# Decoder trunk on one core: sums as columns, each tile evicted at its own last product, the last three groups tile by tile, and the last 1/rms by root, reciprocal and one Newton step

## The chip, the cores and the metric

The kernel runs on one core of a Trainium2 chip. Its engines, as the profile names them, are TensorE (PE, with PEld for its weight loads), VectorE (DVE), ScalarE (ACT), GpSimd (POOL) and SyncE (SP), whose queue issues nearly all DMAs. The metric is the device time of one execution in microseconds (us), as a median of several runs.

## What is computed

Two layers of a decoder trunk over 1024 rows of width 1024, in float32. Each layer has a mixing sub-layer and a SwiGLU sub-layer of width 2816, both between two RMS norms and modulated by a vector c:

```python
c_act = jax.nn.silu(c)
for l in range(DEPTH):
    mod = c_act @ ada_w[l] + ada_b[l]
    shift_m, scale_m, gate_m, shift_f, scale_f, gate_f = [
        m[:, None, :] for m in jnp.split(mod, N_MOD, axis=-1)]

    h = rms_norm(x, g_pre_mix[l]) * (1.0 + scale_m) + shift_m
    proj = h @ w_in[l] + b_in[l]
    q, k, v, u = jnp.split(
        proj, [ATTN_WIDTH, ATTN_WIDTH + KV_WIDTH, ATTN_WIDTH + 2 * KV_WIDTH], axis=-1)
    ...
    mix = jnp.concatenate([attn_out, pool_out], axis=-1) @ w_out[l]
    x = x + gate_m * rms_norm(mix, g_post_mix[l])

    h = rms_norm(x, g_pre_ffn[l]) * (1.0 + scale_f) + shift_f
    f = (jax.nn.silu(h @ w_gate[l]) * (h @ w_up[l])) @ w_down[l]
    x = x + gate_f * rms_norm(f, g_post_ffn[l])
```

q and k are rotated in the first 16 of each head's 64 columns; attention is a sliding window of 128 with a sink per head; u goes through trailing means of 2, 4, 8 and 16 rows.

## The kernel before

**Products.** A float32 product is made of three matmuls of rounded parts: `split` (L220 on ScalarE, L221 on VectorE) makes a high part `hi` and a rest `lo`, and `mm3` multiplies hi by hi (L263), hi by lo (L266) and lo by hi (L267). A full matmul has 512 columns. The rows are worked in two halves of 512, each of four tiles of 128.

**Stages.** Mixing of a layer is u, q and kv products, rotation, attention and pooling, then `natural_proj` for w_out, which for each half of the columns (nh = 0, 1) collects four tiles in four PSUM banks over all k and evicts them at the end (L680: times G, the gate row; and a sum of squares on ScalarE, L501). In the profiled execution it lies at about 30 to 300 us for layer 0 and 985 to 1243 for layer 1. The up products (300 to 700, 1340 to 1600) and the down products (700 to 970, 1600 to 1903) use seven products `p1` to `p7` on combined blocks instead of eight. In the last layer the last down product, `p4`, goes in pairs of tiles, (0, 1) and then (2, 3); each pair runs through six groups of k, and within the last group tile by tile. `ended` is called at each tile's end and, in the last layer, calls `finish`.

**The ada stream.** The modulation `c_act @ ada_w` is spread beside these stages in steps of a few operations: `ada_sum` loads two blocks of ada_w in SP's queue and adds them, times c_act, into a tile `ada` of [128 x 512] on VectorE (L298); what is left is a sum over the 128 partitions. Before the change `ada_gate` (the gate rows: two halves for each sub-layer) and `ada_pair` (shift and scale of the second sub-layer: four parts) split the tile and multiply it by `picks`, a column of ones between zeros, so that the sum comes out as a row. The gate's row gets its bias and norm weight (two rows loaded by DMA; L471, L472) and goes to DRAM, from where `load_gate` spreads it over the partitions as `G`. The pair's rows are copied to SBUF and turned to columns by transposes. `ada_columns`, used for the first sub-layer, makes columns directly: four matmuls of 128 x 128 parts of `ada` by one column of ones (L441).

**Order.** The program is written as generators, which `run` interleaves: at each step of the main stream, so many steps of the others. From that order a scheduler builds each engine's own queue, which that engine then works in order. A DMA is issued when SP's queue gets to it.

**Norms.** `inv_rms` (L274, L275, L279 to L281) makes 1/rms on VectorE from an integer first guess and three Newton steps of three small operations each; L509 adds the two halves' sums of squares before it. `finish` (L648 in the last half) then multiplies the tile by 1/rms, adds the residual and stores it.

Of the kernel before, what the change touches and what calls it, by code (L numbers as in the profile page):

```python
# [11 lines left out]
F32 = mybir.dt.float32  # L12
# [54 lines left out]
def hybrid_decoder_kernel(  # L67
# [33 lines left out]
    SMALL = dict(junk=1, st=12, rs=8, ss=4, halo=8, rows=1, cols=2, colp=4, sk=2)  # L101
    SHARED = dict(hT=8, fn=4, raw=2, hi=3, lo=3, sa=2, sb=2, ar=2, ada=1, ph=3, G=1)
    REGIONS = dict(
        mix=dict(cfa=2, cfb=2, qkv=5, bqkv=1, uT=4, pt=2, vz=5, rt=1, qT=1, pth=2, pwh=1, pwl=1),
# [43 lines left out]
    picks = const.tile([P, 7], F32R, name="picks")  # L148
# [9 lines left out]
    pick_row = t_("rt", [P, 7])  # L158
    nc.vector.memset(pick_row, 0.0)
    nc.vector.memset(pick_row[:, 3:4], 1.0)  # L160
    nc.vector.tensor_copy(picks, pick_row)
# [26 lines left out]
    cos_t = const.tile([P, NB, RH], F32, name="cos_t")  # L188
    sin_t = const.tile([P, NB, RH], F32, name="sin_t")
# [5 lines left out]
    def rotary_angles():  # L195
# [8 lines left out]
        nc.vector.tensor_scalar(sin_t, ang, math.pi, -math.pi, op0=ALU.min, op1=ALU.max)  # L204
        nc.vector.scalar_tensor_tensor(cos_t, sin_t, -1.0, sin_t, op0=ALU.mult, op1=ALU.max)
        nc.vector.tensor_scalar(cos_t, cos_t, -1.0, math.pi / 2.0, op0=ALU.mult, op1=ALU.add)
# [78 lines left out]
    def ada_sum(l, n0, got, whole=False):  # L285
# [23 lines left out]
        if whole:  # L309
            got.append(acc)  # L310
        else:
            got += [t_("ph", [P, 512], F32R), t_("ph", [P, 512], F32R)]
            split(*got, acc)
# [3 lines left out]
    NROW = 6 * KD + 2 * KD + 4 + 4  # L317

    def load_col_rows(l):
        rows = t_("rows", [P, P])[:NROW]  # L320
        r = 0
        for src, n in (
            (ada_b[l], 6 * KD), (g_pre_mix[l], KD), (g_pre_ffn[l], KD),
            (pool_scale[l], 4), (b_in[l, QKV:INW], 4),
        ):
            nc.sync.dma_start(rows[r : r + n, :], src.rearrange("(r p) -> r p", p=P))
            r += n
        return rows

    def cols_of(rows):  # L330
        bank = msc_bank()
        nc.tensor.transpose(bank[:, :NROW], rows, ident[:NROW, :NROW])
        cols = t_("cols", [P, NROW])
        nc.vector.tensor_copy(cols, bank[:, :NROW])
        return cols
# [68 lines left out]
    def ada_pair(l, sub, cols, ab):  # L404

        held = {}

        def close(r, hi, lo):
            if r == 0:
                held["bank"] = msc_bank()  # L410
            dst, pick = held["bank"][0:4, :], picks[:, 3 - r : 7 - r]
            nc.tensor.matmul(dst, pick, hi, start=r == 0, stop=False)
            nc.tensor.matmul(dst, pick, lo, start=False, stop=r == 3)
            if r < 3:
                return
            rows = t_("ar", [P, 512])[0:4]
            nc.scalar.activation(rows, dst, AF.Copy)
            bank = msc_bank()
            for i in range(4):
                nc.tensor.transpose(bank[:, 4 * i : 4 * i + 4], rows[:, i * P : (i + 1) * P], ident[0:4, 0:4])  # L420
            tv = bank[:, 0:16].rearrange("p (i m o) -> p m o i", i=4, m=2)
            for m in range(2):
                k0 = (3 * sub + 1 - m) * KD
                nc.vector.tensor_add(
                    ab[:, m, :].rearrange("p (o i) -> p o i", o=2), tv[:, m],
                    cols[:, k0 : k0 + KD].rearrange("p (o i) -> p o i", o=2),
                )
            ada_scale(ab, sub, slice(0, KD), cols)

        return [  # L430
            (l, (3 * sub + 1 - r // 2) * D + r % 2 * 512, lambda hi, lo, r=r: close(r, hi, lo))
            for r in range(4)
        ]

    def ada_columns(l, sub, cols, ab):


        def close(r, acc):
            bank = msc_bank()
            for i in range(4):  # L440
                nc.tensor.matmul(  # L441
                    bank[:, i : i + 1], acc[:, i * P : (i + 1) * P], ones[:, 0:1], start=True, stop=True
                )
# [7 lines left out]
            (l, (3 * sub + 1 - r // 2) * D + r % 2 * 512, lambda acc, r=r: close(r, acc), True)  # L451
# [5 lines left out]
    def ada_gate(l, sub):  # L457
# [3 lines left out]
        def close(half, hi, lo):  # L461
            n0 = (3 * sub + 2) * D + half * 512
            o = slice(half * 512, half * 512 + 512)
            gb = t_("ar", [P, 512])[0:1]
            gg = t_("ar", [P, 512])[0:1]
            nc.sync.dma_start(gb, ada_b[l : l + 1, n0 : n0 + 512])
            nc.sync.dma_start(gg, (g_post_ffn if sub else g_post_mix)[l : l + 1, o])
            bank = msc_bank()
            nc.tensor.matmul(bank[0:1, :], picks[:, 3:4], hi, start=True, stop=False)
            nc.tensor.matmul(bank[0:1, :], picks[:, 3:4], lo, start=False, stop=True)  # L470
            nc.vector.tensor_add(gb, bank[0:1, :], gb)  # L471
            nc.vector.tensor_mul(gb, gb, gg)  # L472
            nc.sync.dma_start(row[:, o], gb)

        return [
            (l, (3 * sub + 2) * D + half * 512, lambda hi, lo, half=half: close(half, hi, lo))
# [157 lines left out]
    def finish(h, t, fn, ss, G, xt=None):  # L634
# [4 lines left out]
        rstd = inv_rms(ss[:, 2 * t : 2 * t + 2])  # L639
# [13 lines left out]
    def natural_proj(fn, left, wsrc, ss, G):  # L653
# [7 lines left out]
        for nh in range(2):  # L661
            cs = slice(nh * 512, (nh + 1) * 512)
            banks = [acc_bank() for _ in range(NT)]
            for k in range(K):
# [10 lines left out]
                for t in range(NT):  # L675
                    mm3(banks[t], lh[:, tiles[t]], ll[:, tiles[t]], wh, wl, k == 0, k == K - 1)
                yield
            for t in range(NT):
                square_sum(ss, t, nh, banks[t])
                nc.vector.tensor_mul(fn[t][:, cs], banks[t], G[:, cs])  # L680
# [73 lines left out]
    def u_pass(l, h, hT, cols, uts, piece_read, ask):  # L754
        banks = [acc_bank() for _ in range(4)]
        for k in range(KD):
# [5 lines left out]
            yield  # L762
        for g in range(4):
# [10 lines left out]
            uts.append(ut)  # L774

    def att_rotary(blk, qkv):
        rot = qkv[:, 0:QK].rearrange("p (n d) -> p n d", d=HD)
        t1 = rot[:, :, 0:RH]
        t2 = rot[:, :, RH:ROT]
        nr = NH + NKV  # L780
        cb = cos_t[:, blk : blk + 1, :].to_broadcast([P, nr, RH])
        sbc = sin_t[:, blk : blk + 1, :].to_broadcast([P, nr, RH])
        tmp = t_("rt", [P, 4, nr, RH])
        nc.vector.tensor_mul(tmp[:, 0], t1, cb)
        nc.vector.tensor_mul(tmp[:, 1], t2, sbc)
        nc.vector.tensor_mul(tmp[:, 2], t2, cb)
        nc.vector.tensor_mul(tmp[:, 3], t1, sbc)
        nc.vector.tensor_sub(t1, tmp[:, 0], tmp[:, 1])
        nc.vector.tensor_add(t2, tmp[:, 2], tmp[:, 3])
# [444 lines left out]
    def down(l, wd, load, kept, fn, ended, last, prelude):  # L1234
# [47 lines left out]
        def products(name, g, lh, ll, rights, banks, ts, evict):  # L1282
# [3 lines left out]
            for some in [range(n)] if whole else [(i,) for i in range(n)]:  # L1286
                for t in ts:
                    sl = tiles[t - ts[0]]
# [37 lines left out]
        for ts in ((0, 1), (2, 3)) if last else (range(NT),):  # L1326
            banks = {t: acc_bank() for t in ts}
            for g, (p0, p1) in enumerate(DOWN_GROUPS):
# [308 lines left out]
```

## Time and profile before

| | us |
|---|---|
| median of 3 runs | 1912.27 (1906.89, 1912.27, 1913.08) |
| profiled execution | 1915.26 |
| its span | 1913.5 |
| granted clock of TensorE, mean | 0.993 |
| ScalarE busy | 946.4 (49%) |
| moved by DMA | 341.86 MB, mean 179 GB/s |

The span runs from the first to the last event that the profiler saw; the execution's time has a little around it. Busy time is counted by instruction. A matmul's row in the timeline has a duration of 0.39 us, but the next one starts before it ends, so the pitch between starts is what counts. In the views of waits a row names the engine, the tile and line that waited, and behind the arrow the engine, tile and line that it waited for; then the total, the number of waits and the longest. A half-clock stretch is one in which the profile shows the granted clock at 0.50.

### The profile page before, as it was taken

The numbers are of one execution on the slowest core, as the hardware profiler recorded it, in microseconds if no ns is written. First come the engines' busy times: TensorE is split into PE (matmuls) and PEld (weight loads), VectorE is DVE, ScalarE is ACT, GpSimd is POOL, SyncE is SP. The second block draws the span as 40 slices with busy tenths as digits, with TensorE's granted clock in tenths as the row PEclk, the third lists the DMA queues.
The fourth block names the chain that finished last, engine by engine and source line by source line (L and its number), as shares of the span: only waits on it lengthen the run. The fifth ranks groups of instructions, "written<-read, shape, count | busy, mean of one in ns | idle before, by whom it ended". The sixth has DMA issues, their size and how long they took to land.

```text
span 1913.5 us, 26037 instructions
## 1 busy us (share of the span) xinstructions
PE 1866.0 (98%) x8954; PEld 1541.1 (81%) x8954; DVE 1541.9 (81%) x2913; ACT 946.4 (49%) x1786; POOL 20.4 (1%) x67
## 2 busy tenths in 40 slices
PE   7999999999999999999999989999999999999997
PEld 5887788888878788888888868888887887888886
DVE  7899886678788888788878988846888888877687
ACT  4875795553222223445548667845622222244452
POOL 0000000000000000000000000000000000000000
PEclk9999999999999999999999989999999999999999
DMA  9345563555555655944554464536754566574342
GB/s 343 108 144 161 160 220 127 187 182 192 183 180 187 206 206 172 320 144 149 175 175 138 125 179 165 177 110 211 218 181 149 197 211 201 198 251 150 114 152 102
DMA packets 229540, 341.86 MB, mean 179 GB/s; under 512 B 17016, under 2 KB 126472, under 8 KB 229408
## 3 DMA queue, kind: packets, MB, share of 16 engines
q1 hardware_dynamic: 228800, 338.10, 53.6%
q10 hardware_dynamic: 576, 2.10, 0.3%
q8 instruction: 70, 1.15, 0.2%
q14 instruction: 62, 0.51, 0.1%
q0 software_dynamic: 32, 0.00, 0.0%
HBM read 267.25 MB, written 72.89 MB: 178 GB/s over the span
## 4 chain that ended last, share of the span: by engine, by line
PE 77%; DVE 12%; DMA 5%; ACT 3%; issue 2%; SPq 0%; DVEq 0%; ACTq 0%; POOL 0%; POOLq 0%
PE acc L263 24%; PE acc L266 23%; PE acc L267 23%; DMA ar<-in_ada_w_dram 2%; DVE lo L221 2%; DMA raw<-in_w_up_dram 2%; DVE ada L298 1%; PE msc L893 1%; PE msc L561 1%; ACT hi L220 1%; DVE fn L1151 1%; PE pv L263 1%; PE pv L266 1%; ACT raw L554 1%; DMA ar<-x 1%
## 5 line engine op out<-in xcount | busy, mean ns | idle before, releaser
L220 ACT ACTIVATE hi<-raw 128x1024 fp32r<-128x1024 f32 (+1 forms) x388 | 331.9, 868 | 364.9 <-PE acc L266 198.8
L221 DVE TENSOR_TENSOR lo<-raw,hi 128x1024 fp32r<-128x1024 f32 (+1 forms) x388 | 379.9, 986 | 121.6 <-ACT hi L220 117.4
L263 PE MATMUL acc<-t,hi 128*128 128x512 f32 x704 | 275.1, 391 | 5.8 <-ACT hi L220 5.8
L266 PE MATMUL acc<-t,hi 128*128 128x512 f32 x704 | 274.7, 390 | 0.0
L267 PE MATMUL acc<-t,lo 128*128 128x512 f32 x704 | 272.1, 390 | 0.1
L263 PE MATMUL acc<-bh,hi 128*128 128x512 f32 x520 | 202.9, 390 | 0.0
L267 PE MATMUL acc<-bh,lo 128*128 128x512 f32 x520 | 202.4, 389 | 0.0
L263 PE MATMUL acc<-hT,hi 128*128 128x512 f32 x480 | 190.2, 396 | 0.6 <-DVE fn L680 0.6
L266 PE MATMUL acc<-hT,hi 128*128 128x512 f32 x480 | 188.4, 393 | 0.0
L267 PE MATMUL acc<-hT,lo 128*128 128x512 f32 x480 | 187.5, 391 | 0.0
L1151 DVE TENSOR_TENSOR fn<-acc,fn 128x512 f32<-128x512 f32 x220 | 150.3, 684 | 39.4 <-PE acc L267 39.1
L263 PEld LDWEIGHTS acc<-t,hi 128*128 128x128 f32 x704 | 132.4, 188 | 35.3 <-ACT hi L220 8.2
L267 PEld LDWEIGHTS acc<-t,lo 128*128 128x128 f32 x704 | 132.4, 188 | 29.3 <-DVE lo L221 1.5
L266 PEld LDWEIGHTS acc<-t,hi 128*128 128x128 f32 x704 | 132.5, 188 | 27.2
L266 PE MATMUL acc<-ph,hi 128*128 128x512 f32 x320 | 124.7, 390 | 0.0
L1087 ACT ACTIVATE fn<-fn 128x512 f32<-128x512 f32 x44 | 27.8, 633 | 185.7 <-DVE fn L1151 185.7
L298 DVE SCALAR_TENSOR_TENSOR ada<-ar,c_act,ada 128x512 f32<-128x512 f32 x140 | 104.5, 746 | 12.5 <-DMA ar<-in_ada_w_dram 11.3
L267 PEld LDWEIGHTS acc<-bh,lo 128*128 128x128 f32 x520 | 97.6, 188 | 20.4
L263 PEld LDWEIGHTS acc<-bh,hi 128*128 128x128 f32 x520 | 97.6, 188 | 20.2 <-ACT sb L1249 0.2
L263 PE MATMUL acc<-hi 128*128 128x512 f32 x256 | 103.6, 410 | 2.4 <-DVE fn L680 2.0
L263 PEld LDWEIGHTS acc<-hT,hi 128*128 128x128 f32 x480 | 90.2, 188 | 19.2 <-DVE fn L680 1.4
L267 PEld LDWEIGHTS acc<-hT,lo 128*128 128x128 f32 x480 | 90.1, 188 | 18.6 <-issue 0.2
(315 smaller groups left out, 3813.5 us busy)
## 6 DMA issues: line engine op xcount, KB each, us to landing
ar<-in_ada_w_dram SPq DMA_DIRECT2D x160, 256.0 KB
raw<-in_w_gate_dram SPq DMA_DIRECT2D x44, 512.0 KB
raw<-in_w_up_dram SPq DMA_DIRECT2D x44, 512.0 KB
raw<-in_w_in_dram SPq DMA_DIRECT2D x80, 256.0 KB
raw<-keeps SPq DMA_DIRECT2D x40, 512.0 KB
keeps<-fn SPq DMA_DIRECT2D x66, 256.0 KB
two_b<-in_w_down_dram SPq DMA_DIRECT2D x30, 512.0 KB
raw<-keepa SPq DMA_DIRECT2D x25, 512.0 KB
```

Of the source, the lines that this page charges most:

```text
L220: a = nc.scalar.activation(hi, src, AF.Copy)
L221: v = nc.vector.tensor_sub(lo, src, hi.bitcast(F32))
L263: ins = nc.tensor.matmul(dst, lh, rh, start=first, stop=False)
L266: nc.tensor.matmul(dst, lh, rl, start=False, stop=False)
L267: return nc.tensor.matmul(dst, ll, rh, start=False, stop=last)
L298: ins = nc.vector.scalar_tensor_tensor(acc, w, c_act[:, i : i + 1], acc, op0=ALU.mult, op1=ALU.add)
L554: nc.scalar.activation(hf, bank, AF.Identity, bias=shift, scale=scale)
L561: ins = nc.tensor.transpose(bank[:, t * P : (t + 1) * P], src[t], ident)
L893: nc.tensor.transpose(bank[:, i * P : (i + 1) * P], s[:, ii, ck * P : (ck + 1) * P], ident)
L1087: nc.scalar.activation(g, g, AF.Silu)
L1151: nc.vector.tensor_add(halves_of(dst)[m], bank, halves_of(src)[m])
```

## The change

1. **Sums as columns.** `ada_gate` and the second sub-layer's parts now use `column_sums` (the four one-column matmuls). The gate's bias and norm weight come as columns out of `cols`, which grows by 16 rows; the product is a [128 x 4] tile `gc`, written to the DRAM row by a DMA whose elements are of 4 bytes. `picks`, `ada_pair`, its transposes and the gate's two row loads go. `ada_stream` calls a part's closing one step later than before.
2. **Evictions.** `natural_proj` evicts each tile right behind its own last product; `u_pass` evicts ahead of its last step's end.
3. **Rotation.** Two products of [128 x 10 x 16] and two sums instead of four products of [128 x 10 x 8] and two sums; the tables of sine and cosine hold each value twice. `vz` has four buffers instead of five.
4. **The last product.** In the last layer the last three groups of each pair of tiles run tile by tile.
5. **The last 1/rms.** In the last half the first column half's share, with epsilon, is prepared ahead (`ahead`); `inv_rms_ahead` takes a root on ScalarE, a reciprocal and one Newton step on VectorE.

```diff
+    def column_sums(acc):
+        bank = msc_bank()
+        for i in range(4):
+            nc.tensor.matmul(
+                bank[:, i : i + 1], acc[:, i * P : (i + 1) * P], ones[:, 0:1], start=True, stop=True
+            )
+        return bank[:, 0:4]
...
-        def close(half, hi, lo):
-            n0 = (3 * sub + 2) * D + half * 512
-            o = slice(half * 512, half * 512 + 512)
-            gb = t_("ar", [P, 512])[0:1]
-            gg = t_("ar", [P, 512])[0:1]
-            nc.sync.dma_start(gb, ada_b[l : l + 1, n0 : n0 + 512])
-            nc.sync.dma_start(gg, (g_post_ffn if sub else g_post_mix)[l : l + 1, o])
-            bank = msc_bank()
-            nc.tensor.matmul(bank[0:1, :], picks[:, 3:4], hi, start=True, stop=False)
-            nc.tensor.matmul(bank[0:1, :], picks[:, 3:4], lo, start=False, stop=True)
-            nc.vector.tensor_add(gb, bank[0:1, :], gb)
-            nc.vector.tensor_mul(gb, gb, gg)
-            nc.sync.dma_start(row[:, o], gb)
+        def close(half, acc):
+            bank = column_sums(acc)
+            k0 = (3 * sub + 2) * KD + 4 * half
+            g0 = 8 * KD + 8 + sub * KD + 4 * half
+            gc = t_("gc", [P, 8])[:, 0:4]
+            nc.vector.tensor_add(gc, bank, cols[:, k0 : k0 + 4])
+            nc.vector.tensor_mul(gc, gc, cols[:, g0 : g0 + 4])
+            nc.sync.dma_start(row[0, half * 512 : half * 512 + 512].rearrange("(i p) -> p i", p=P), gc)
...
     def ada_stream(jobs):
-        for l, n0, close, *whole in jobs:
+        ending = None
+        for l, n0, close in jobs:
             got = []
-            yield from ada_sum(l, n0, got, *whole)
-            close(*got)
+            for i, _ in enumerate(ada_sum(l, n0, got)):
+                yield
+                if ending and i == 0:
+                    ending()
+            ending = lambda close=close, got=got: close(*got)
+        yield
+        if ending:
+            ending()
...
                 for t in range(NT):
                     mm3(banks[t], lh[:, tiles[t]], ll[:, tiles[t]], wh, wl, k == 0, k == K - 1)
+                    if k == K - 1:
+                        square_sum(ss, t, nh, banks[t])
+                        nc.vector.tensor_mul(fn[t][:, cs], banks[t], G[:, cs])
                 yield
-            for t in range(NT):
-                square_sum(ss, t, nh, banks[t])
-                nc.vector.tensor_mul(fn[t][:, cs], banks[t], G[:, cs])
...
+        rot = qkv[:, 0:QK].rearrange("p (n d) -> p n d", d=HD)[:, :, 0:ROT]
...
+        tmp = t_("rt", [P, 2, nr, ROT])
+        nc.vector.tensor_mul(tmp[:, 0], rot, cb)
+        nc.vector.tensor_mul(tmp[:, 1], rot, sbc)
...
-                products(name, g, lh, ll, kept4[g], banks, ts, evict)
+                if last and g >= len(DOWN_GROUPS) - 3:
+                    final.append((g, lh, ll))
+                else:
+                    products(name, g, lh, ll, kept4[g], banks, ts, evict)
                 for _ in range(n):
                     yield
+
+            for t in ts:
+                for g, lh, ll in final:
+                    products(name, g, lh, ll, kept4[g], banks, (t,), evict, ts[0])
...
+    def inv_rms_ahead(s0, ahead):
+        a, r, y, z = (t_("rs", [P, 8])[:, :1] for _ in range(4))
+        nc.vector.scalar_tensor_tensor(a, s0, 1.0 / D, ahead, op0=ALU.mult, op1=ALU.add)
+        nc.scalar.activation(r, a, AF.Sqrt)
+        nc.vector.reciprocal(y, r)
+        nc.vector.scalar_tensor_tensor(z, y, -0.5, a, op0=ALU.mult, op1=ALU.mult)
+        nc.vector.tensor_mul(z, z, y)
+        nc.vector.scalar_tensor_tensor(y, z, 1.5, y, op0=ALU.add, op1=ALU.mult)
+        return y
```

Three places in VectorE's queue, in the kernel's line numbers before and after. Removed lines shift the numbers: L298 becomes L296, L680 becomes L661, L221 becomes L219, L1151, L1172 and L1196 become L1136, L1157 and L1181, L1571 becomes L1569, and L648 becomes L630.

The first is the end of the program, from the eviction of the last pair of tiles on (`sb` is the tile, `ss` the sums of squares, `rs` the small tiles of 1/rms). Before:

```order
L1246 TENSOR_TENSOR sb<-acc,sb 128x512 x2
L1571 TENSOR_TENSOR sb<-sb,G 128x512
L509 TENSOR_REDUCE rs<-ss 128x1
L274 TENSOR_SCALAR rs<-rs 128x1
L1571 TENSOR_TENSOR sb<-sb,G 128x512
L275 TENSOR_SCALAR rs<-rs 128x1
L279 SCALAR_TENSOR_TENSOR rs<-rs 128x1
L509 TENSOR_REDUCE rs<-ss 128x1
L280 TENSOR_TENSOR rs<-rs 128x1
L274 TENSOR_SCALAR rs<-rs 128x1
L281 SCALAR_TENSOR_TENSOR rs<-rs 128x1
```

After, the last tile, behind the last operation of the tile ahead of it:

```order
L630 SCALAR_TENSOR_TENSOR sb<-sb,rs,hT 128x512 x2
L1231 TENSOR_TENSOR sb<-acc,sb 128x512
L1569 TENSOR_TENSOR sb<-sb,G 128x512
L608 SCALAR_TENSOR_TENSOR rs<-ss,st 128x1
L610 RECIPROCAL rs<-rs 128x1
L611 SCALAR_TENSOR_TENSOR rs<-rs 128x1
L612 TENSOR_TENSOR rs<-rs 128x1
L613 SCALAR_TENSOR_TENSOR rs<-rs 128x1
L630 SCALAR_TENSOR_TENSOR sb<-sb,rs,hT 128x512 x2
```

The two tiles' small operations stood in turns; now one tile is complete before the other's eviction, and five small operations stand between eviction and last product.

The second is the change from nh = 0 to nh = 1 in layer 1's `natural_proj` (`fn` is the evicted tile, `acc` the PSUM bank, L298 a step of the ada stream, L843 and L219 parts of attention). Before:

```order
L221 TENSOR_TENSOR ph<-msc,pth 128x512
L298 SCALAR_TENSOR_TENSOR ada<-ar,c_act,ada 128x512
L832 TENSOR_TENSOR hi<-qkv,hi 128x4x64
L680 TENSOR_TENSOR fn<-acc,G 128x512 x2
L298 SCALAR_TENSOR_TENSOR ada<-ar,c_act,ada 128x512
L680 TENSOR_TENSOR fn<-acc,G 128x512
L298 SCALAR_TENSOR_TENSOR ada<-ar,c_act,ada 128x512
L680 TENSOR_TENSOR fn<-acc,G 128x512
L221 TENSOR_TENSOR lo<-raw,hi 128x512
```

After (L415 adds the bias to four columns that the ones make):

```order
L296 SCALAR_TENSOR_TENSOR ada<-ar,c_act,ada 128x512
L661 TENSOR_TENSOR fn<-acc,G 128x512
L415 TENSOR_TENSOR colp<-msc,cols 128x4
L661 TENSOR_TENSOR fn<-acc,G 128x512
L294 TENSOR_SCALAR ada<-ar,c_act 128x512
L843 ISA sb,st<-msc,mask 128x256
L843 ISA st 128x1
L843 ISA sb,st<-msc,mask 128x256
L843 ISA st 128x1
L219 TENSOR_TENSOR ph<-msc,pth 128x512
L296 SCALAR_TENSOR_TENSOR ada<-ar,c_act,ada 128x512
L661 TENSOR_TENSOR fn<-acc,G 128x512 x2
```

The first two evictions now stand ahead of an ada step and of a block of attention, and the last two behind it.

The third is the second half of the gate in layer 0's up stage (L1151 adds a product's bank to a tile, L1172 combines a block of weights in `raw`). Before:

```order
L298 SCALAR_TENSOR_TENSOR ada<-ar,c_act,ada 128x512
L1088 TENSOR_TENSOR fn<-fn 128x512
L1172 TENSOR_TENSOR raw<-raw 128x8x128
L1196 TENSOR_TENSOR fn<-fn 128x512
L1151 TENSOR_TENSOR fn<-acc,fn 128x512
L221 TENSOR_TENSOR ph<-ada,ph 128x512
```

After:

```order
L296 SCALAR_TENSOR_TENSOR ada<-ar,c_act,ada 128x512
L1073 TENSOR_TENSOR fn<-fn 128x512
L1136 TENSOR_TENSOR fn<-acc,fn 128x512
L1181 TENSOR_TENSOR fn<-fn 128x512
L1157 TENSOR_TENSOR raw<-raw 128x8x128
L1136 TENSOR_TENSOR fn<-acc,fn 128x512
L435 TENSOR_TENSOR gc<-msc,cols 128x4
L436 TENSOR_TENSOR gc<-gc,cols 128x4
```

L1181 and one L1136 have moved ahead of L1157, and the split of the sum (L221) is gone; the two small operations of the gate stand a place later.

More of the change, by code (lines that the diff above doesn't have):

```diff
@@ L185, in hybrid_decoder_kernel @@
     nc.scalar.activation(c_act, c_raw, AF.Silu)
-    cos_t = const.tile([P, NB, RH], F32, name="cos_t")
-    sin_t = const.tile([P, NB, RH], F32, name="sin_t")
+    cos_t = const.tile([P, NB, 2, RH], F32, name="cos_t")
+    sin_t = const.tile([P, NB, 2, RH], F32, name="sin_t")
     ang = t_("pt", [P, NB, RH])
@@ L308, in ada_sum @@
                 yield
[L309 to L313, printed above, removed]
+        got.append(acc)
         yield
-    NROW = 6 * KD + 2 * KD + 4 + 4
+    NROW = 6 * KD + 2 * KD + 4 + 4 + 2 * KD
     def load_col_rows(l):
@@ L1556, in hybrid_decoder_kernel @@
         ss = [t_("ss", [P, 8]) for _ in range(NHALF)]
-        tail = []
+        tail, aheads = [], []
         def ended(name, t):
```

106 lines of the change are left out of this document (39 added, 67 removed).

## The prediction

> **What bounds the kernel now.** I read the page's busy shares first.
>
> ```profile
> PE 1866.0 (98%) x8954; PEld 1541.1 (81%) x8954; DVE 1541.9 (81%) x2913; ACT 946.4 (49%) x1786; POOL 20.4 (1%) x67
> ```
>
> TensorE is busy for 98% of the span, so work taken off another engine pays only where TensorE stands still or runs slower. Next come the view of TensorE's waits (total, times, longest) and the windows of the two mixing stages in which the ada stream runs (us, PE, PEld, DVE, ACT, POOL busy, granted clock, DMA).
>
> ```profile
> PE msc L332 <- DVE ident L152: 11.1, 1, 11.1
> PE acc L263 <- ACT hi L220: 6.1, 5, 2.1
> PE msc L893 <- DVE sb L883: 3.8, 7, 0.9
> PE acc L263 <- DVE fn L680: 2.6, 5, 0.8
> PE msc L412 <- ACT ph L220: 1.9, 2, 1.8
> PE msc L814 <- DVE rt L787: 1.7, 1, 1.7
> PE msc L835 <- DVE fn L680: 1.4, 1, 1.4
> ```
>
> ```profile
> 157.00:200.00 43.00, 38.45 (x187) 29.83 (x186) 39.41 (x101) 26.25 (x61) 0.79 (x2) 0.92 0.59 172
> 1098.00:1142.00 44.00, 39.17 (x184) 30.34 (x184) 40.56 (x104) 27.80 (x69) 1.35 (x2) 0.91 0.59 173
> ```
>
> The waits are short and spread. In the two windows VectorE is busier than TensorE, 39.41 and 40.56 us, and the clock falls to 0.92 and 0.91. The same windows cut small, of TensorE alone, show why:
>
> ```profile
> 164.76:168.17 3.41, 3.31 (x13) 0.50 0.49 141
> 195.48:198.89 3.41, 2.94 (x10) 0.50 0.45 111
> 536.81:540.22 3.41, 3.41 (x9) 0.50 0.03 4
> 1106.84:1110.25 3.41, 3.41 (x10) 0.50 0.55 159
> 1137.56:1144.38 6.82, 6.01 (x15) 0.50 0.64 174
> 646.00:650.00 4.00, 2.86 (x13) 1.00 0.57 197
> ```
>
> Stretches of 3.41 us run at half clock, one after each of the longest waits (L412, L680, a first gate's L220, L814, L835), the one at 1137.56 twice as long. Each 3.41 us costs 1.7. At 646, where TensorE stood still for 1.14 of 4 us, the clock stayed 1.00: a stall of about 1.4 is near the point from which half clock follows.
>
> **The change part by part.** The sum is against the profiled execution, 1915.26 us (span 1913.5), 3.0 above the median 1912.27; the difference is then carried to the median.
>
> *The tail.* The timeline after the last matmuls (start, duration):
>
> ```profile
> 1902.24 0.39 PE L266 MATMUL acc<-two_b,hi 128*128 128x512 f32 x1
> 1902.47 0.39 PE L267 MATMUL acc<-two_b,lo 128*128 128x512 f32 x1
> 1902.90 0.69 DVE L1246 TENSOR_TENSOR sb<-acc,sb 128x512 f32<-128x512 f32 x1 [0.67 <-PE acc L267]
> 1903.68 0.63 ACT L501 ACTIVATE junk<-sb 128x512 bf16<-128x512 f32 x1 [0.64 <-DVE sb L1246]
> 1904.22 0.19 ACT L501 ACTIVATION_READ_ACCUMULATOR junk<-sb 128x1 f32 x1
> ...
> 1908.31 0.15 DVE L279 SCALAR_TENSOR_TENSOR rs<-rs 128x1 f32<-128x1 f32 x1
> 1908.50 0.16 DVE L280 TENSOR_TENSOR rs<-rs 128x1 f32<-128x1 f32 x1
> 1908.89 1.42 DVE L648 SCALAR_TENSOR_TENSOR sb<-sb,rs,hT 128x512 f32<-128x512 f32 x2
> ```
>
> ```profile
> L874 ACT ACTIVATE st<-st 128x4 f32<-128x4 f32 x32 | 6.5, 203 | 2.2 <-DVE st L873 1.9
> ```
>
> Matmuls follow each other at 0.23. The sum of squares is read out at 1904.41, the last product ends at 1910.31, and between them lie the small operations of two tiles, 0.19 apart. After: three hand-offs between engines of 0.09 (add's end 1903.59 to square 1903.68), five small DVE operations at 0.19, a root at 0.20 (the 128x4 ACT row), then 1.42: 1904.41 + 0.27 + 0.95 + 0.20 + 1.42 = 1907.25, 3.1 earlier. The other tile's last product ends 18 matmuls (six products of three), 4.1 us, ahead instead of six, 1.4, so its own chain of about 4.4 ends some 0.3 after the last matmul and can delay the last add; I take **−2.7** (bounds −3.1, and 0 if the two chains still meet). The root needs a table load, which has one row here:
>
> ```profile
> L185 ACT ACT_TABLE_LOAD x1 | 1.3, 1283 | 7.3 <-DMA rows<-in_g_pre_ffn_dram 7.3
> ```
>
> It falls at the first root, two tiles earlier, hidden by TensorE's matmuls; uncovered it costs 1.3.
>
> *TensorE's work.* The picks go: 32 matmuls of 512 columns at 0.23 are 7.3 us. 64 one-column matmuls come, priced by the like ones of the first modulation, a row of the chain:
>
> ```profile
> 790.86 0.79 PE msc L441 x8
> ```
>
> 0.099 each, 6.3 in all: **−1.0**, with the small transposes that go too.
>
> *The mixing stages.* VectorE and ScalarE lose the split of each ada sum and the two row operations of each gate:
>
> ```profile
> L221 DVE TENSOR_TENSOR ph<-ada,ph 128x512 fp32r<-128x512 f32 x16 | 11.0, 685 | 0.9 <-ACT ph L220 0.7
> L471 DVE TENSOR_TENSOR ar<-msc,ar 1x512 f32<-1x512 f32 x8 | 5.4, 674 | 0.8 <-PE msc L470 0.8
> ```
>
> A gate half on VectorE was 0.69 + 2 × 0.67 (L472 is as large as L471) = 2.03 and becomes two small operations, 0.38: 1.65 less. What reaches the end is the waits. L412's longest is 1.8; its sums now need no cast, but the new matmuls stand directly behind the same products, so part of the hand-off stays: **−1.5** (0 to −1.9). The evictions of mix_out at 1134:
>
> ```profile
> 1134.52 1.28 DVE L680 TENSOR_TENSOR fn<-acc,G 128x512 f32<-128x512 f32 x2
> 1135.72 0.74 DVE L298 SCALAR_TENSOR_TENSOR ada<-ar,c_act,ada 128x512 f32<-128x512 f32 x1
> ```
>
> Two such ada steps, 0.7 each, stand between the four evictions (the order shows the second, behind the third eviction), for which TensorE waits 2.6 + 1.4 (L263 and L835 on L680). After, each tile is evicted as soon as its own last product is done, while the next tile's three matmuls (0.69) run; in layer 1 attention work still stands between. I take half, **−2.0** (0 to −4.0). If the stalls fall below about 1.4, the half-clock stretches behind them go: of five in mixing (the double one counted as two) I take two, **−3.4** (0 to −8.5). The rotation's four products before L814's wait are these:
>
> ```profile
> 1101.83 0.24 DVE L784 TENSOR_TENSOR rt<-qkv,cos_t 128x80 f32<-128x80 f32 x1
> 1101.98 0.23 DVE L785 TENSOR_TENSOR rt<-qkv,sin_t 128x80 f32<-128x80 f32 x1
> ```
>
> Four at 0.15 become two of double width, some 0.23 each by the slope to the 0.69 of 512 columns, and two sums a piece follow unchanged: **−0.4** at L814 (0 to −1.7). A loss at these places would need a new wait, and the order shows new ones only at the write and in the up stages, below. VectorE's relief of some 5 us per stage (two gate halves at 1.65 and part of four splits at 0.69) also shortens other short waits (L893's 3.8): **−0.8** (0 to −3.8). The earlier u eviction hides in L263's wait and the vz buffer less beside TensorE's work; both nothing.
>
> The Trainium skill, "TensorE: Matmul & The Clock Gate", section "HAM oscillation — how this bites in real kernels", gives as its rule "no PE-idle gaps >~3.4µs". By it no stall here, the longest being 2.1, would cost clock, the sum would lose its −3.4 and give −4.5, 1907.8. The trace disagrees: half-clock stretches stand behind stalls of 1.4 to 2.1.
>
> *The gate write.* Four halves in mixing, whose write to DRAM was one row and becomes 512 elements of 4 bytes:
>
> ```profile
> 129.74 1.44 DMA gate<-ar
> DVE pos_f L196 <- DMA pos_i<-in_positions_dram: 5.3, 1, 5.3
> 136.00 0.75 DVE L298 SCALAR_TENSOR_TENSOR ada<-ar,c_act,ada 128x512 f32<-128x512 f32 x1 [1.10 <-DMA ar<-in_ada_w_dram]
> ```
>
> The order puts it on SP's queue ahead of the next ada load, so VectorE's wait of 1.10 grows; VectorE saves 1.65 there. I take +0.25 a half, **+1.0** (0 by the relief; 5.3, the 4-byte position load's wait, less 1.44, +3.9 a half, by the nearest small-element row). The Trainium skill, "DMA: Bandwidth & Descriptors", "Specifications", wants transfers of at least 512 B, since below that the engines do read-modify-write. It speaks against this edit; this trace has no 4-byte write.
>
> *The up stages.* At the second gate:
>
> ```profile
> 646.60 0.68 DVE L1196 TENSOR_TENSOR fn<-fn 128x512 f32<-128x512 f32 x1
> 647.21 0.68 DVE L1151 TENSOR_TENSOR fn<-acc,fn 128x512 f32<-128x512 f32 x1
> ```
>
> L1172 (now L1157), just ahead of these, prepares weights whose split TensorE waits for. L1196 and L1151, 0.61 apart, move ahead of it: 1.2 in each layer, **+2.4** (0 if the wait has slack, +5.8 if each stall also costs 1.7 of clock). The first gate's order is unchanged.
>
> *The head.* Four more small DVE operations before ident, for which TensorE waits 11.1:
>
> ```profile
> 10.78 0.22 DVE L152 CAST ident<-G 128x128 fp32r<-128x128 f32 x1
> ```
>
> Four half as wide as this row, which is 0.22, overlapping in part: I take **+0.5** (0.4, half of each, to 0.9, all of it); nothing covers them.
>
> *The sum:* +0.5 − 2.7 − 1.0 − 1.5 − 2.0 − 3.4 − 0.4 − 0.8 + 1.0 + 2.4 = −7.9: 1907.4 against the profiled execution, **1904.4** against the median.
>
> **The rivals.** *S, the waits only move:* VectorE stays near 40 of 43 us and another short wait takes each place; only tail, head and TensorE's work come in: −2.7 + 0.5 − 1.0 = −3.2, with +2.4 up to −0.8: 1911.5. *G, all of it:* the stalls of L412, L814 and L680/L835 and all five half-clock stretches go. For it: each stretch has its stall. −1.9 − 1.7 − 4.0 − 8.5, less tail and work 3.2, plus 2.4 is −16.9 to −20: about 1895. *L, slower:* the 4-byte write holds SP's queue for the time of the position load, +3.9 at two of four mixing halves, and the up stage's later weights cost clock too, +5.8, against −3.2 with no mixing gain: about +10.6, 1923. It decides from a write of 3.1 us, today's 1.44 and VectorE's relief of 1.65.
>
> **How the numbers follow.**
> The forecast has 0.50, S 0.30, G 0.10, L 0.10. S is strong because VectorE was the releaser of most waits and stays busy; G needs every hand-off to work; L needs a price that no row shows. The forecast's own range is 1898 (four windows go) to 1909 (none, and the up stage costs more). The range reaches from G's edge to S with the spread of the runs: 1894 to 1914; L is left out, and a tenth at the edges. Measurement tells 0.3%, 5.7 us, from no change: faster means below 1906.5. That is G, most of the forecast (0.39 of 0.50) and a little of S (0.03): 0.52. Same: the rest of the forecast and S, 0.38. Slower: L, 0.10.
>
> **What would show it.** Tail: last matmul to last product 4.7 us instead of 7.45, with no table load behind the last matmul. Mixing: L412's wait gone, and no row after 1.8 from the new sums; TensorE's waits on the evictions under 2; fewer stretches at 0.50 in 157–200 and 1098–1142, PEclk there above 0.92. Gate write: its landing time on the chain, and VectorE's longest wait for an ada load, 1.10 now; over 3 is L. Up: TensorE's stalls near 646 and its twin in layer 1 longer by 1.2; half clock behind them adds 1.7 each. Head: ident 0.5 later. The prediction is wrong if the half-clock stretches stay in number though the waits before them shrink, or if new ones come in the up or down stages, or if the write is over 3 us.

## The result

The changed kernel took 1940.7 us (median of 4 runs, 1939.44 to 1942.17); before, beside it, 1910.18. The ratio is 1.0161, with a 95% interval of 1.0138 to 1.0183: 30.5 us slower, where 1904.4 was forecast. Its profiled execution has a span of 1937.7 us at a mean granted clock of 0.989.

The page's busy times, and the view of TensorE's waits, of the changed kernel (line numbers are up to 38 lower than before; L261, L264, L265 are the three matmuls of a product):

```profile
PE 1878.3 (97%) x9042; PEld 1558.4 (80%) x9042; DVE 1523.6 (79%) x2848; ACT 937.1 (48%) x1773; POOL 19.4 (1%) x67
PE msc L878 <- DVE sb L868: 12.9, 7, 6.0
PE acc L261 <- ACT hi L218: 7.9, 7, 2.6
PE msc L878 <- DVE st L843: 4.2, 1, 4.2
PE msc L799 <- DVE hi L794: 2.6, 2, 1.4
```

VectorE and ScalarE have less to do, as expected, and TensorE is busy for longer, 1878 us instead of 1866. But attention's transpositions (L878), which waited 0.9 at most, now wait 6.0 and 4.2 for VectorE. VectorE in turn waits for data, and SP for the gate write (the views of VectorE's and SP's waits):

```profile
DVE ada L296 <- DMA ar<-in_ada_w_dram: 28.3, 24, 5.9
DVE raw L1151 <- DMA raw<-in_w_up_dram: 23.2, 14, 7.4
SPq L446 <- DMA gate<-gc: 24.9, 4, 7.9
```

Before, the first two were these, and SP's waits for a gate write came to 2.9 us, 0.8 at most:

```profile
DVE ada L298 <- DMA ar<-in_ada_w_dram: 11.3, 18, 1.3
DVE raw L1166 <- DMA raw<-in_w_up_dram: 11.5, 7, 2.7
```

One such place, layer 1's first gate half, in the chain (start, duration, what) and in windows (us, TensorE busy, clock, DMA share, GB/s). The gate write (L437) is issued at 1043.94, an ada load right behind it:

```profile
1042.11 0.80 PE msc L403 x8
...
1044.43 9.88 DMA ar<-in_ada_w_dram
```

```profile
1040.00:1045.00 5.00, 5.00 (x35) 1.00 0.45 141
1046.00:1054.00 8.00, 5.37 (x33) 1.00 0.57 40
```

For 8 us the core's whole traffic falls from 141 to 40 GB/s while its DMA engines are busy for more of the time (0.57 instead of 0.45). A load of 256 KB takes 9.88 us, where the median of the 160 ada loads is 3.3, and TensorE stands still for 2.63 of 8 us. It is the place where rival L has its loss; the price is the question.

### The profile page after: what moved, and what is told of

It is laid out like the page before. It is cut to its first block, busy times and chain, and to the rows that moved or that the text cites. A ratio compares the mean times of both kernels' runs of the same rounds, so it can differ in the third digit from the quotient of the medians.

```text
span 1937.7 us, 26100 instructions
## 1 busy us (share of the span) xinstructions
PE 1878.3 (97%) x9042; PEld 1558.4 (80%) x9042; DVE 1523.6 (79%) x2848; ACT 937.1 (48%) x1773; POOL 19.4 (1%) x67
## 4 chain that ended last, share of the span: by engine, by line
PE 76%; DVE 11%; DMA 7%; ACT 3%; issue 2%; SPq 1%; DVEq 0%; ACTq 0%; POOL 0%; POOLq 0%
PE acc L261 23%; PE acc L265 23%; PE acc L264 23%; DMA raw<-in_w_up_dram 3%; DMA ar<-in_ada_w_dram 2%; DVE lo L219 2%; PE msc L878 1%; ACT hi L218 1%; PE msc L532 1%; DVE ada L296 1%; DVE fn L1136 1%; DMA ar<-x 1%; PE msc L403 1%; PE pv L261 1%; PE pv L264 1%
## 5 line engine op out<-in xcount | busy, mean ns | idle before, releaser
L219 DVE TENSOR_TENSOR lo<-raw,hi 128x1024 fp32r<-128x1024 f32 (+1 forms) x388 | 380.3, 986 | 121.1 <-ACT hi L218 118.5
L261 PE MATMUL acc<-t,hi 128*128 128x512 f32 x704 | 277.0, 394 | 7.2 <-ACT hi L218 7.2
L265 PE MATMUL acc<-t,lo 128*128 128x512 f32 x704 | 274.8, 393 | 2.7 <-DVE lo L219 2.6
L264 PE MATMUL acc<-t,hi 128*128 128x512 f32 x704 | 275.8, 392 | 0.0
L261 PE MATMUL acc<-bh,hi 128*128 128x512 f32 x520 | 202.9, 390 | 0.0
L265 PE MATMUL acc<-bh,lo 128*128 128x512 f32 x520 | 202.5, 389 | 0.0
L261 PE MATMUL acc<-hT,hi 128*128 128x512 f32 x480 | 190.9, 398 | 2.5 <-ACT uT L749 2.0
L264 PE MATMUL acc<-hT,hi 128*128 128x512 f32 x480 | 188.3, 392 | 0.0
L265 PE MATMUL acc<-hT,lo 128*128 128x512 f32 x480 | 187.8, 392 | 0.0
L1136 DVE TENSOR_TENSOR fn<-acc,fn 128x512 f32<-128x512 f32 x220 | 150.2, 683 | 42.7 <-PE acc L265 42.3
L261 PEld LDWEIGHTS acc<-t,hi 128*128 128x128 f32 x704 | 133.3, 189 | 36.9 <-ACT hi L218 9.8
L265 PEld LDWEIGHTS acc<-t,lo 128*128 128x128 f32 x704 | 133.3, 189 | 32.8 <-DVE lo L219 4.9
L264 PEld LDWEIGHTS acc<-t,hi 128*128 128x128 f32 x704 | 133.3, 189 | 27.7
L296 DVE SCALAR_TENSOR_TENSOR ada<-ar,c_act,ada 128x512 f32<-128x512 f32 x140 | 104.5, 746 | 28.8 <-DMA ar<-in_ada_w_dram 28.3
L264 PE MATMUL acc<-ph,hi 128*128 128x512 f32 x320 | 124.7, 390 | 0.0
L265 PEld LDWEIGHTS acc<-bh,lo 128*128 128x128 f32 x520 | 97.7, 188 | 20.3
L261 PEld LDWEIGHTS acc<-bh,hi 128*128 128x128 f32 x520 | 97.7, 188 | 20.0
L261 PEld LDWEIGHTS acc<-hT,hi 128*128 128x128 f32 x480 | 90.4, 188 | 21.0 <-ACT uT L749 2.4
L265 PEld LDWEIGHTS acc<-hT,lo 128*128 128x128 f32 x480 | 90.1, 188 | 18.6
L264 PEld LDWEIGHTS acc<-hT,hi 128*128 128x128 f32 x480 | 90.4, 188 | 16.4
```

Of the source, the lines that this page charges most:

```text
L219: v = nc.vector.tensor_sub(lo, src, hi.bitcast(F32))
L261: ins = nc.tensor.matmul(dst, lh, rh, start=first, stop=False)
L264: nc.tensor.matmul(dst, lh, rl, start=False, stop=False)
L265: return nc.tensor.matmul(dst, ll, rh, start=False, stop=last)
L296: ins = nc.vector.scalar_tensor_tensor(acc, w, c_act[:, i : i + 1], acc, op0=ALU.mult, op1=ALU.add)
L1136: nc.vector.tensor_add(halves_of(dst)[m], bank, halves_of(src)[m])
```

## The experiments

Each run is compared with the kernel before on the same chip. The times are medians; the ratio on record can differ a little from their quotient (for e6 0.9977 against 0.9982):

| run | us | before beside it | ratio (95%) |
|---|---|---|---|
| change | 1940.7 | 1910.18 | 1.0161 (1.0138 to 1.0183) |
| e1 gate as rows | 1911.74 | 1909.07 | 1.0015 (1.0006 to 1.0025) |
| e2 write on ScalarE's queue | 1944.65 | 1909.07 | 1.0176 (1.0153 to 1.0198) |
| e3 elements of 16 B | 1913.56 | 1909.07 | 1.0025 (1.0011 to 1.0039) |
| e4 write twice | 1949.14 | 1909.07 | 1.0207 (1.0192 to 1.0222) |
| e5 all but the columns | 1907.19 | 1910.0 | 0.9981 (0.9972 to 0.9991) |
| e6 tail only | 1906.54 | 1910.0 | 0.9977 (0.9967 to 0.9986) |
| e7 columns only, gate as rows | 1913.2 | 1910.0 | 1.0015 (1.0006 to 1.0024) |
| e9 e1 and a spare write, near | 1935.1 | 1910.59 | 1.0128 (1.0110 to 1.0147) |
| e10 e1 and a spare write, far | 1911.92 | 1910.59 | 1.0014 (1.0000 to 1.0029) |
| e11 tail, late picks | 1911.68 | 1910.59 | 1.0006 (0.9996 to 1.0016) |
| e12 e5, late picks | 1912.79 | 1910.59 | 1.0017 (1.0007 to 1.0026) |
| e13 e1, closing at once | 1918.94 | 1909.4 | 1.0051 (1.0035 to 1.0066) |
| e14 tail and rotation | 1905.07 | 1909.4 | 0.9977 (0.9967 to 0.9987) |
| e15 tail and evictions | 1908.53 | 1909.4 | 0.9994 (0.9986 to 1.0003) |

### The gate write: e1 to e4

```diff
-            nc.sync.dma_start(row[...].rearrange("(i p) -> p i", p=P), gc)
+            # e1, one step of the stream later
+            nc.tensor.transpose(bank[0:4, 0:P], gc, ident)
+            nc.scalar.activation(gr, bank[0:4, 0:P], AF.Copy)
+            nc.sync.dma_start(row[...].rearrange("(i p) -> i p", p=P), gr)
+            # e2
+            nc.scalar.dma_start(row[...].rearrange("(i p) -> p i", p=P), gc)
+            # e3
+            nc.sync.dma_start(row[...].rearrange("(p i) -> p i", i=4), gc)
+            # e4
+            nc.sync.dma_start(row[...].rearrange("(i p) -> p i", p=P), gc)
+            nc.sync.dma_start(spare[...].rearrange("(i p) -> p i", p=P), gc)
```

> The changed kernel, with the gate's four columns turned back into rows (one transposition on TensorE, one copy on ScalarE, a step of the ada stream later), so that each half goes to DRAM as 4 elements of 512 B instead of 512 of 4 B. Theory W (the write of 4-byte elements holds back the core's DMAs for about 8 us, eight times): the stalls and half-clock stretches at 112, 671, 1051, 1087 and 1608 to 1634 us, some 36 us with their clock, go; 1902 to 1910 us. Theory O (the new order of VectorE's work and the later closings make the loss, the write only marks the places): within 4 us of the changed kernel, 1936 to 1942.

> The changed kernel, with the 4-byte write issued from ScalarE's queue instead of SP's. Theory W1 (the write slows all transfers of the core while it lasts): ada and weight loads are as late as before, DMA falls to some 20 GB/s for about 7 us after each write, 1933 to 1942 us. Theory W2 (only what is queued behind the write on the same queue waits for it): the mixing stalls go and only the G loads' own wait for the write in the two up stages stays, 1905 to 1920 us. Theory O: 1936 to 1942.

> The changed kernel, with the gate written as 128 elements of 16 B for each half instead of 512 of 4 B; the gate's columns then stand in another order, so the output is that of a permuted gate. Theory W, priced by the element: a write takes about 2 us of held transfers instead of 8, 1906 to 1916 us. Theory W, priced by what an element of under 512 B costs at all (a fixed latency): near the changed kernel, 1930 to 1942. Theory O: 1936 to 1942.

> The changed kernel, with each 4-byte write made a second time into a spare row of DRAM. Theory W: the slow stretch after each write grows from about 8 to about 16 us; at least as much again is lost as the writes cost now, 1965 to 1990 us. Theory O: only a little more traffic, 1938 to 1946.

e1 takes 29.0 us off (1940.7 to 1911.74; 27.9 by the ratios), 1.7 above theory W's range, and theory O falls. e2 keeps the whole loss (1944.65, 2.7 above every range it was given): another queue does not help, so it isn't what stands behind the write on SP's queue. Its traffic falls as in the change:

```profile
1040.00:1045.00 5.00, 5.00 (x35) 1.00 0.42 134
1046.00:1054.00 8.00, 6.75 (x38) 1.00 0.23 34
```

Its engines are busy for only 0.23 of the second window, so part of that fall is that less was asked for; but its ada load takes 9.18 us there, much as in the change. e3 is near e1: 128 elements of 16 B cost little. e4 misses: a second write adds 8.4 us, not 30. Its trace shows why: the two writes are issued 0.44 us apart (1050.35 and 1050.79), and the ada load behind them takes 11.13 us instead of 9.88. They overlap, and the slow stretch grows by little.

### What in the write is slow: e9 and e10

Both are e1, with a write that nothing reads:

```diff
             nc.vector.tensor_mul(gc, gc, cols[:, g0 : g0 + 4])
+            # e9
+            nc.sync.dma_start(spare[0:512].rearrange("(i p) -> p i", p=P), gc)
+            # e10
+            nc.sync.dma_start(spare.rearrange("(i p s) -> p i s", p=P, s=64)[:, :, 0], gc)
```

> The first experiment's kernel (gate as rows, 1911.7 us) with one thing added: each gate half's columns are also written as 512 elements of 4 B, side by side, into a spare row that nothing reads. Theory W1 (such a write slows all transfers of the core while it lasts): most of the loss comes back although no G load waits for it, 1925 to 1938 us. If the loss came from the G loads that waited for the write on SP's queue: 1912 to 1918.

> As the run beside it, but the 512 elements stand 256 B apart in the spare buffer. Theory L (neighbouring elements lie in the same line of memory, and partial writes to one line wait for each other): the write is harmless, 1911 to 1916 us. Theory C (each small element costs its time wherever it goes): as the run beside it, within 4 us.

e9 brings 23.4 us of the loss back (1935.1 against 1911.74; 21.6 by the ratios) though no G load waits for it. e10 moves the same 512 elements of 4 B, 256 B apart, in as many DMA packets (233845 on both pages), and its median has no cost that can be measured, though four of its ten runs took 1916 to 1922 us where e1's highest is 1914.6. Windows from some 2 us after the first write on and behind layer 1's first write, of e9 and then of e10:

```profile
109.00:117.00 8.00, 5.16 (x31) 1.00 0.61 39
1046.00:1054.00 8.00, 5.80 (x35) 1.00 0.61 45
```

```profile
106.80:114.80 8.00, 8.00 (x52) 1.00 0.75 224
1034.80:1042.80 8.00, 8.00 (x49) 1.00 0.63 182
```

The same windows behind the other writes agree: at seven of the eight e10 moves 180 to 244 GB/s, where e9 moves 38 to 63 and the change 9 to 61. At the eighth, layer 0's second half in mixing, e10 too moves only 34, with its DMA engines busy for 0.13: little is asked for there.

So 512 elements of 4 B do not by themselves hold the traffic back; they do where neighbours go to neighbouring addresses, and e3 shows that a quarter as many, four times as large, do so far less. That they meet in one line of memory and wait for each other there was argued, not shown: the runs show that the distance decides, not where the wait is, and no distance between 4 and 256 B was tried.

### The columns, and a second trace of before: e5, e7, e8

e5 has the parts 2 to 5 of the change on the kernel before (but five `vz` buffers still), e7 has part 1 with the write of e1 and the four `vz` buffers, and e8 is the kernel before.

> The kernel before with all of the change but the sums as columns: evictions, rotation, tail. Theory P (a sum as columns costs TensorE 0.8 us, since the trace shows eight records for one closing and not two closings: 16 closings are 13 us against 7.3 for the picks that go, some +6 to +8 net, and that ate what the other parts give): 1901 to 1906 us where before is about 1909. Theory N (the columns are worth as much in waits as they cost, and the other parts give nothing but the tail): 1906 to 1908.

> The kernel before with the sums as columns alone, the gate written as rows of 512 B (as in the first experiment). Theory P: TensorE's one-column matmuls add some 15 us and the picks' 7.3 go, waits fall by some 3 to 4: 1912 to 1916 us. Theory N: 1908 to 1911.

> The kernel before once more, for a second trace. If the half-clock stretches of mixing belong to fixed stalls, they stand at the same places (165, 195, 537, 1107, 1138 us); if they depend on where a stall falls against the clock's own windows, some are gone or elsewhere, the execution is nearer to 1909 than the 1915.26 that was profiled, and the sum that was made against the profiled execution counted a chance as a gain.

e7 is where theory P has it, 2.9 us slower (0.15% of 1910; one of its 12 runs took 10672.91 us, which does not move the median); e5 is where theory N has it, 3.6 us faster and no more than the tail alone (e6, below). So the columns do cost, and the other parts bring nothing beside the tail. The two do not add up: e1, which has all parts, is at 1.0015 as e7 is, so beside the columns the 3.6 us of the other parts do not show. Against e5 the columns cost 6.5 us (1.0015 less 0.9981), and why it is 2.9 in one place and 6.5 in the other was not found. The chain's row of the changed kernel above has eight matmul records for one closing of four sums, and its groups of instructions have this row:

```profile
L403 PE MATMUL msc<-ones_r,ada 128*128 128x1 f32 x160 | 19.2, 242 | 1.3 <-DVE ada L296 1.3
```

Of the 160 records 32 are layer 1's first modulation, as before; 128 are new, where 64 were forecast.

e8 shows the other error. Windows as in the prediction, of TensorE alone (e8, then before's at its first gate):

```profile
157.00:200.00 43.00, 37.77 (x185) 1.00 0.61 178
525.00:545.00 20.00, 18.65 (x82) 1.00 0.58 195
1098.00:1142.00 44.00, 38.35 (x177) 0.96 0.63 182
...
1134.56:1137.97 3.41, 3.40 (x8) 0.50 0.57 149
```

```profile
525.00:545.00 20.00, 17.88 (x72) 0.91 0.41 135
```

The same program, with nearly the same stalls in the two mixing windows (at the first gate TensorE stands still for 1.35 us instead of 2.12), has one half-clock stretch ahead of its last matmul in this trace (1134.56), where the first trace had the time of six. Its span is 1908.6 us, 4.9 less.

### The other parts alone: e6, e14, e15

```diff
# e6: only inv_rms_ahead, ahead, final and t0 of the change
# e14: e6, and the rotation's tables and operations
# e15: e6, and in natural_proj
                 for t in range(NT):
                     mm3(banks[t], lh[:, tiles[t]], ll[:, tiles[t]], wh, wl, k == 0, k == K - 1)
+                    if k == K - 1:
+                        square_sum(ss, t, nh, banks[t])
+                        nc.vector.tensor_mul(fn[t][:, cs], banks[t], G[:, cs])
```

> The kernel before with the tail alone: the last three groups tile by tile, and 1/rms by root, reciprocal and one Newton step. Both theories: from last matmul's start to the span's end 8.9 us instead of 11.0, so 2.1 us less, 1906 to 1908 us; a regrouping that cost TensorE a wait would give 1909 or more.

> The kernel before with the tail and the rotation in four operations. If the rotation gives what the prediction said (0.4 us) or nothing: 1905.5 to 1908, not to be told from the tail alone. If it gives more and the evictions take it back: 1901 to 1905.

> The kernel before with the tail and each tile of the output product evicted at its own last product. If the evictions give nothing: 1905 to 1908.5 us. If they cost what the rotation gives: 1908 to 1911. If they give the 2 us and half-clock stretches of the prediction: 1900 to 1904.

The tail gives 0.23% (2.7 to 6.3 us), the rotation nothing beside it by the ratios (its median lies between its two ranges), and the evictions take 3.2 back (0.9994 less 0.9977, of 1910; the one interval begins where the other ends, so this is just clear of the noise). The timeline of VectorE in e15 at layer 0's change from nh = 0 to nh = 1, and then in e6:

```profile
191.66 0.75 DVE L298 SCALAR_TENSOR_TENSOR ada<-ar,c_act,ada 128x512 f32<-128x512 f32 x1
192.33 0.42 DVE L820 TENSOR_TENSOR hi<-qkv,hi 128x256 fp32r<-128x256 f32 x1
192.91 0.75 DVE L298 SCALAR_TENSOR_TENSOR ada<-ar,c_act,ada 128x512 f32<-128x512 f32 x1 [0.16 <-DMA ar<-in_ada_w_dram]
193.58 2.48 DVE L690 TENSOR_TENSOR fn<-acc,G 128x512 f32<-128x512 f32 x4
...
195.97 0.74 DVE L298 SCALAR_TENSOR_TENSOR ada<-ar,c_act,ada 128x512 f32<-128x512 f32 x1
```

```profile
191.30 1.28 DVE L691 TENSOR_TENSOR fn<-acc,G 128x512 f32<-128x512 f32 x2
192.50 0.74 DVE L298 SCALAR_TENSOR_TENSOR ada<-ar,c_act,ada 128x512 f32<-128x512 f32 x1
```

In e15 ScalarE's square of the first bank starts at 191.65, so the bank is done, but VectorE comes to it at 193.58, behind two ada steps that stand ahead of it in its queue. The evictions are in one piece and no earlier. The view of TensorE's waits of e15 has them:

```profile
PE acc L263 <- DVE fn L690: 2.8, 4, 1.9
```

In e6 the like row has the same total, 2.8, over five waits of at most 0.8; here the longest is 1.9. This shows why nothing was gained; the loss itself is spread over e15's trace in pieces of 1 to 2 us, and was not traced to one wait.

### When a sum is closed: e11 to e13

```diff
# e11 (e6), e12 (e5): split one step later, picks another step later
+            for i, _ in enumerate(ada_sum(l, n0, got)):
+                yield
+                if rest:
+                    rest()
+                    rest = None
+                if ending and i == 0:
+                    rest = ending()
# e13 (e1): no delay
-                if ending and i == 0:
-                    write = ending()
+            write = close(*got)
```

> The tail alone (1906.5 us) and the closings of the ada sums spread over two later steps: the split one step later, the picks another step later, the sums still as rows. If the five stalls of 1.0 to 1.8 us at the closings (160, 643, 1470 and the like) come from work that reaches the engines' queues right behind the sum: 1900 to 1904 us. If VectorE's load sets them, they move: 1905 to 1908.

> All of the change but the columns (1907.2 us), with the same late split and picks. If evictions and rotation give something once the closings no longer stall: 1898 to 1902 us, under the run beside it. If they give nothing, as they did without it: within 2 us of the run beside it.

> The first experiment's kernel (all of the change, gate as rows, 1911.7 us) with each sum closed as soon as it is complete, as before the change, instead of one step later. If the late closing costs the columns what it cost the picks: 1905 to 1908 us. If not: 1910 to 1914.

e11 and e13 miss; e12 stays within 2 us of e11. By the ratios, closing later costs the picks 5.5 and 6.9 us (e11 against e6, 1.0006 less 0.9977; e12 against e5, 1.0017 less 0.9981), and closing at once costs the columns 6.9 (e13 against e1, 1.0051 less 1.0015). In e11 TensorE waits 2.8 us for the split of the late sums, and the two waits are up to 1.7 long:

```profile
PE msc L466 <- DVE ph L221: 2.8, 2, 1.7
```

The change's own delay was right for the columns. Why it is worth that much was not followed further.

## Why the prediction was wrong

**The gate write: +1.0 forecast, 28 to 29 measured.** The step that failed is "I take +0.25 a half". It priced the write by how long its own successor waits and set VectorE's relief against it, and its upper end was the position load, 5.3 us. e2 and e9 show that the write slows the core's transfers for about 8 us, and not just what is queued behind it. The eight halves reach TensorE at five places (112, 672, 1051, 1087 and 1634 us), where the prediction counted four halves in mixing and none in the up stages. Of the 28.1 us that the change's span is above e1's, TensorE stands still for 17.5 (59.4 against 41.9) and is busy for 10.6 more (1878.3 against 1867.7), at mean granted clocks of 0.989 and 0.995: the four longest of these stalls are each followed by a stretch at half clock, which the prediction's term for the write did not have either. The G load waits for the write at all four sub-layers, 5.1 to 7.9 us each, and in the up stages it holds the loads of w_gate and w_up, on SP's queue behind it:

```profile
649.80 0.37 SPq L437 DMA_DIRECT2D gate<-gc  x1
658.10 0.32 SPq L446 DMA_DIRECT2D G<-gate  x1
658.52 0.39 SPq L1119 DMA_DIRECT2D raw<-in_w_gate_dram  x1
```

That may be the 5.6 us that are left of the loss (29.0 less e9's 23.4; 6.3 by the ratios), which no run has by itself. Rival L had the right edit and place, and its sign came in: VectorE's longest wait for an ada load is 5.9 us, over 3. But it had only 0.10, its time was 18 too low, and its mechanism, that the write holds SP's queue, is not the one: e2 loses as much from ScalarE's queue. That "this trace has no 4-byte write" should have given the edit a wide range. The Trainium skill, "DMA: Bandwidth & Descriptors", "Specifications", has transfers under 512 B done by read-modify-write. e10 agrees only in part: 512 elements of 4 B, 256 B apart, have no cost that its median shows.

**TensorE's work: −1.0 forecast, +5.5.** The row "790.86 0.79 PE msc L441 x8" was read as two closings; it is one, with two records for each sum. 128 records at 0.10 are 12.8 us, less 7.3 for the picks: +5.5. The whole of part 1 measures +2.9 (e7) or +6.5 (e1 against e5), so whether the columns earn anything back in waits stays open.

**Waits at the closings: −1.5 forecast, and VectorE's relief, −0.8.** L412's wait of 1.9 is gone and the new matmuls wait 1.3, no row of them over 1.8, as the prediction's sign has it:

```profile
PE msc L403 <- DVE ada L296: 1.3, 2, 1.0
```

That is 0.6 less in this trace; in e1's they wait 0.4, which is 1.5 less. No run has either term by itself.

**Half-clock stretches: −3.4 forecast, nothing to earn.** The profiled execution, 1915.26, lay above all 19 runs of before in the first experiments' comparison (1905.35 to 1911.42), and five stretches in mixing were part of that. e8 has stalls at 160, 190, 1098 and 1132 us too, with one stretch, and e1 still has the time of four in mixing (at 165, at 195, twice as long, and at 1107). They were priced as if each belonged to its stall; by these two traces a stall only risks one. The Trainium skill ("TensorE: Matmul & The Clock Gate", "HAM oscillation — how this bites in real kernels") has as its rule that TensorE's gaps stay under some 3.4 us. Neither trace fits it, since e8's one stretch also stands behind stalls under 2 us (waits of 0.76 and 0.99).

**Evictions: −2.0 forecast, +3.2** (e15 against e6). The step "each tile is evicted as soon as its own last product is done" took each eviction to come as soon as the code has it; at run time VectorE's queue was behind. In the change itself TensorE's waits on the evictions are 1.3 us where they were 4.0, under 2 as the prediction's sign has it, and no time came of it.

**Rotation: −0.4 forecast, 0** by the ratios (e14 against e6), inside what can be told.

**Up stages: +2.4 forecast, about 0.** Without the write (e1) the stall at 645 is there, 1.7 us instead of 1.1 before, but the one at 1586, 1.3 before, is gone. In the change it is there, at 1608, just ahead of the last write.

**Tail: −2.7 forecast; the mechanism right, 2.05 in the trace.** Before, last matmul's start to last product's end is 1910.31 − 1902.47 = 7.84. After, it is 1934.53 − 1928.74 = 5.79 (from that matmul's end 5.40, where the prediction has 4.7):

```profile
1928.44 1.41 DVE L630 SCALAR_TENSOR_TENSOR sb<-sb,rs,hT 128x512 f32<-128x512 f32 x2
1928.74 0.39 PE L265 MATMUL acc<-two_b,lo 128*128 128x512 f32 x1
1929.77 0.68 DVE L1231 TENSOR_TENSOR sb<-acc,sb 128x512 f32<-128x512 f32 x1
...
1931.30 0.69 DVE L1569 TENSOR_TENSOR sb<-sb,G 128x512 f32<-128x512 f32 x1 [0.85 <-ACT junk L472]
1931.91 0.15 DVE L608 SCALAR_TENSOR_TENSOR rs<-ss,st 128x1 f32<-128x1 f32 x1
1932.33 0.16 DVE L610 RECIPROCAL rs<-rs 128x1 f32<-128x1 f32 x1 [0.27 <-ACT rs L609]
...
1933.11 1.42 DVE L630 SCALAR_TENSOR_TENSOR sb<-sb,rs,hT 128x512 f32<-128x512 f32 x2
```

Two things are later than the sum has them. The last add (L1231) starts 1.03 behind the last matmul's start instead of 0.43, behind the other tile's last product (L630), a delay that the prediction named and took too small. And the working left out that L1569 overwrites the tile that the square reads, so it waits for the square, and stands ahead of L608 in VectorE's queue: some 0.6 more. The root's table load is at 1913.15, well ahead of the last matmul, as forecast. The tail's gain, 3.5 us between the medians and 4.4 by the ratio, is more than the trace's 2.05; its interval begins at 2.7, and where the rest is from was not found.

**Head: +0.5 forecast.** TensorE's first wait, for ident, is 11.2 us instead of 11.1, and 10.7 to 11.6 over the runs; it can't be told.

**Two sums of the rivals** are a little off: L's terms make +10.4, not +10.6, and G's reach −19.3, not −20.

The parts that were worth making are the tail (e6) and, at no cost, the rotation (e14): both 0.23% faster than before, 1.8% faster than the change.

## What to carry to other kernels

A column of results that goes to DRAM as neighbouring 4-byte elements can hold up the whole core's traffic; turn it into rows on TensorE first, or into fewer and larger elements (a spread row that is read afterwards was not run), and look at the GB/s in windows behind a new small write before believing anything else. Count the records of one closing in the trace against the instructions in the code before pricing an operation by a row with "x8". Take a second trace of the kernel before, when the profiled execution is above the median: what is only in one of them is no gain to be had.

## What was not expected of the hardware

512 writes of 4 B side by side cut the core's DMA traffic for some 8 us, whichever queue issues them: to 34 to 45 GB/s in the windows shown, where the same 512 writes 256 B apart left it at 182 and 224. 128 writes of 16 B side by side cost 1.8 us in all (e3 against e1). Four one-column float32 matmuls leave eight records and take 0.80 us, as much as three and a half full ones of 512 columns at 0.23.
